# Ten elementwise instructions of the first stage move to GpSimd: four weight sums and six squares

## The chip, the cores and the metric

The kernel runs on one core of a Trainium2 chip. Such a core has five engines that work side by side, each through its own list of instructions in order: TensorE (PE, with its weight loads PEld), VectorE (DVE), ScalarE (ACT), GpSimd (POOL) and SyncE (SP), which here only issues transfers. They meet through semaphores. Operands lie in SBUF (on-chip memory, 128 partitions) or in PSUM, into which PE writes. The metric is the time of one execution on the device in microseconds (us).

## The reference

A decoder trunk of two layers on 512 tokens of width 1024, float32, each layer being `h += 0.5*FFN1(rms(h)); h += Mixer(rms(h)); h += 0.5*FFN2(rms(h))`, and a last normalisation. The first mixer is attention beside a convolution, the second a gated DeltaNet. The part that matters is the very first feed-forward network and its normalisation:

```
def rms_norm(x, g):
    y = xf * lax.rsqrt(jnp.mean(xf * xf, axis=-1, keepdims=True) + NORM_EPS)
    return (y * g).astype(x.dtype)

def swiglu_ffn(h, w_in, w_out):
    gate, up = jnp.split(h @ w_in, 2, axis=-1)
    return (jax.nn.silu(gate) * up) @ w_out
```

with `w_in` of 1024 x 5632 and `w_out` of 2816 x 1024.

## The kernel before

**Layout.** The input stands transposed, features on partitions: `h[d]`, d = 0..7, is a tile of 128 features x 512 tokens. The factor 1/rms of a token (`R`) is multiplied in after the first product, so the product with the weights can start before it is known; only the gain is multiplied in before.

**Split products.** PE multiplies in a faster format (fp32r), and to keep float32 accuracy each operand is split into a rounded part (hi, made by ACT) and a remainder (lo = value - hi, made by DVE). A product takes three matmuls: hi*hi, hi*lo, lo*hi (`mm3`, lines 144 to 146). Weights are split in `wsplit`: ACT makes `whi` (line 120), DVE `wlo` (line 121).

**Fewer products by sums.** A feed-forward network's first product is computed in seven block products where eight would be usual, from sums of blocks (Strassen-Winograd). The sums of x blocks are made in `Norm.sums`, the sums of weight blocks in `sums12` and `sums34`, once for each of the 22 iterations f of the loop over `block(f)`; those of f+1 while f is multiplied. For the first network the weights of f = 0 are fetched ahead, among the x tiles, into four tiles named `raw_pre`, and `sums12(0)` and `sums34(0)` run in the first stage. Each makes two 128x512 instructions, lines 399, 400 and 405, 406, on DVE. They form a chain: 405 needs 400, and 406 needs 399 and 405. ACT needs the result of 405 for its second `whi`, whose `wlo` follows on DVE.

**The first stage**, `Norm.start`, takes the x tiles in four pairs k (d = 2k even, 2k+1 odd):

- ACT multiplies in the gain (`gain`, line 249): `xe` from the even tile, `xo` from the odd one.
- DVE makes sums of 128x256 blocks (lines 256, 260, 262, 263).
- ACT rounds to `xh` (line 271; 128x512 for the even, 128x1280 for the odd tile), DVE subtracts to `xl` (line 276).
- ACT squares `h[d]` into a temporary tile (line 230): tag `a` with two buffers for even d, tag `sq` with one buffer for odd d. PE sums the square over its partitions (line 232, four matmuls of one column for each tile), for 1/rms.
- PE runs ten small matmuls (`warm`, line 209), for the first three pairs, whose result is not used.

Between the pairs `step(ahead)` runs pieces of the first network's generator: the `wsplit`s of f = 0, `sums12(0)` and `sums34(0)`. Then `block(0)` follows, in which `scale` turns the sums into 1/rms.

**What sets the order.** The lists of PE, ACT and DVE in the first stage and in the network's loop are ordered by the code (`manual_schedule`); POOL's and SP's, and all lists in the mixers, are ordered by a scheduler when the program is built. The tile pools add waits: a buffer is written again only when its readers are through. The buffers of `raw_pre` are taken next by the fetches for f = 1, and the pool of the x parts `xe` and `xo` gives its memory to the third weight tile of f = 1.

## Time and profile before

| | |
|---|---|
| median of 3 runs | 2079.42 us (2076.62 to 2080.59) |
| the profiled execution | 2078.23 us |
| its span, first to last instruction | 2076.5 us |
| mean granted TensorE clock | 0.979 |
| mean of a square, ACT line 230 (128x512), 8 of them in the first stage | 615 and 616 ns |
| mean of a weight sum, DVE lines 399, 400, 405, 406 (128x512) | 684 to 692 ns |
| mean of `xl` on DVE, 128x512 and 128x1280 | 686 and 1492 ns |
| mean of `xh` on ACT, 128x512 and 128x1280 | 626 and 1258 ns |
| DVE waits in the first 32.4 us | 3.1 us for `xh`, 2.6 us for the first `xe`, 1.8 us for `whi` |

A profile row of instructions in order of time reads: start, length (us), engine, line, operation, output<-inputs, shape, count, and in brackets the idle time of the engine ahead of it and what ended it. Instructions of one engine overlap a little, since the next begins while the last one drains; the distance from start to start tells what one costs in a row of them. A group's row has the busy time, then the mean in ns, then idle time and releasers. Buffer numbers are left out of names.

### The profile page before, as it was taken

To read this page: it belongs to the slowest core of one execution; us is meant where nothing else is said; L and a number is where in the kernel's file an instruction comes from. 1 tells how busy PE (TensorE), PEld (TensorE's weight loads), DVE (VectorE), ACT (ScalarE), POOL (GpSimd) and SP (SyncE) were. 2 spreads that over 40 slices of the span, in tenths; PEclk is the share of its full clock that TensorE was granted. 3 is DMA by queue.
4 is the path that set the end of the run, shared out by engine and by line. 5 is a ranking of instruction groups with operands and counts; after the bars stand their busy time and mean duration, and the time that the engine had idled before them with its cause. 6 is when DMAs were issued, how large, how long until landed. Compare 5 with 4: busy or idle time off the path is not lost.

```text
span 2076.5 us, 32975 instructions
## 1 busy us (share of the span) xinstructions
PE 2006.1 (97%) x12692; PEld 1774.8 (85%) x12692; DVE 1610.2 (78%) x2761; ACT 1114.4 (54%) x1985; POOL 134.0 (6%) x191
## 2 busy tenths in 40 slices
PE   7999999999999999999999999979989999999997
PEld 6999997786578999987999998767778888999986
DVE  7888879797568888889888888657685578888876
ACT  6444457546654444465444446686454754444455
POOL 0000000110000000000000000233312220000000
PEclk9999999999799999999999999989989999999998
DMA  4333332784043333322333332679634563333321
GB/s 138 111 103 106 103 101 93 178 193 93 21 107 115 108 104 102 97 87 83 113 105 102 102 102 83 180 220 233 140 117 122 122 142 107 103 105 108 98 86 46
DMA packets 108845, 237.70 MB, mean 114 GB/s; under 512 B 22160, under 2 KB 24976, under 8 KB 108688
## 3 DMA queue, kind: packets, MB, share of 16 engines
q1 hardware_dynamic: 90544, 193.06, 30.2%
q0 software_dynamic: 17616, 42.02, 10.8%
q8 instruction: 99, 1.62, 0.3%
q10 hardware_dynamic: 528, 0.52, 0.1%
q14 instruction: 58, 0.48, 0.1%
HBM read 224.55 MB, written 11.01 MB: 113 GB/s over the span
## 4 chain that ended last, share of the span: by engine, by line
PE 80%; DVE 10%; issue 5%; ACT 3%; DMA 2%; SPq 0%; POOL 0%; DVEq 0%; ACTq 0%; POOLq 0%
PE mm L145 12%; PE mm L146 12%; PE mm L144 12%; PE sc L145 7%; PE sc L144 7%; PE sc L146 7%; PE po L146 2%; PE po L145 2%; PE po L144 2%; PE tr L144 2%; PE tr L146 2%; PE tr L145 2%; DVE wlo L121 1%; DVE gl L433 1%; DVE sb L1227 1%
## 5 line engine op out<-in xcount | busy, mean ns | idle before, releaser
L121 DVE TENSOR_TENSOR wlo<-raw,whi 128x1024 fp32r<-128x1024 f32 (+1 forms) x400 | 473.7, 1202 | 158.4 <-ACT whi L120 154.3
L144 PE MATMUL mm<-xh,whi 128*128 128x256 f32 (+2 forms) x1800 | 559.2, 311 | 5.4 <-ACT b L469 3.0
L146 PE MATMUL mm<-xh,wlo 128*128 128x256 f32 (+2 forms) x1800 | 555.5, 309 | 3.3 <-DMA wlo<-in_wgdn 3.3
L145 PE MATMUL mm<-xl,whi 128*128 128x256 f32 (+2 forms) x1800 | 553.9, 308 | 0.8 <-DVE xl L276 0.8
L120 ACT ACTIVATE whi<-raw 128x1024 fp32r<-128x1024 f32 (+1 forms) x400 | 404.8, 1034 | 40.8 <-issue 14.4
L144 PEld LDWEIGHTS mm<-xh,whi 128*128 128x128 f32 (+1 forms) x1800 | 342.0, 190 | 38.4 <-ACT b L469 5.6
L145 PEld LDWEIGHTS mm<-xl,whi 128*128 128x128 f32 (+1 forms) x1800 | 341.7, 190 | 27.4 <-DVE xl L276 1.3
L146 PEld LDWEIGHTS mm<-xh,wlo 128*128 128x128 f32 (+1 forms) x1800 | 342.0, 190 | 20.4 <-DMA wlo<-in_wgdn 3.7
L144 PE MATMUL sc<-xh,whi 128*128 128x256 f32 x1056 | 299.4, 283 | 7.9 <-DVE b L505 7.9
L145 PE MATMUL sc<-xl,whi 128*128 128x256 f32 x1056 | 298.3, 283 | 0.0
L146 PE MATMUL sc<-xh,wlo 128*128 128x256 f32 x1056 | 298.2, 282 | 0.0
L144 PEld LDWEIGHTS sc<-xh,whi 128*128 128x128 f32 x1056 | 201.9, 191 | 9.6 <-DVE b L505 9.6
L433 DVE TENSOR_TENSOR gl<-g,gh 128x512 fp32r<-128x512 f32 (+1 forms) x286 | 179.2, 647 | 32.2 <-ACT gh L432 29.9
L432 ACT ACTIVATE gh<-g 128x512 fp32r<-128x512 f32 (+1 forms) x286 | 166.3, 592 | 67.1 <-PE mm L145 34.8
L146 PEld LDWEIGHTS sc<-xh,wlo 128*128 128x128 f32 x1056 | 202.0, 191 | 0.0
L145 PEld LDWEIGHTS sc<-xl,whi 128*128 128x128 f32 x1056 | 202.0, 191 | 0.0
L450 ACT ACTIVATE a<-a 128x512 f32<-128x512 f32 x88 | 55.6, 632 | 256.8 <-DVE a L449 256.8
L130 ACT ACTIVATE whi<-raw 128x512 fp32r<-128x512 f32 (+2 forms) x109 | 77.1, 735 | 97.1 <-PE mm L145 70.7
L486 ACT ACTIVATE b<-mm 128x256 f32<-128x256 f32 x88 | 33.8, 384 | 162.7 <-PE mm L146 162.7
L501 ACT ACTIVATE b<-mm 128x256 f32<-128x256 f32 x88 | 33.8, 385 | 136.9 <-PE mm L146 136.9
L145 PE MATMUL mm<-gl,whi 128*128 128x512 f32 (+1 forms) x220 | 82.8, 376 | 4.9 <-DVE gl L433 4.7
L826 DVE SCALAR_TENSOR_TENSOR cv<-pad,prm_t,cv 128x512 f32<-128x512 f32 x120 | 84.0, 755 | 0.8
(421 smaller groups left out, 3538.5 us busy)
## 6 DMA issues: line engine op xcount, KB each, us to landing
raw<-in_wf1i SPq DMA_DIRECT2D x82, 512.0 KB, 3.5
raw<-in_wf2i SPq DMA_DIRECT2D x82, 512.0 KB, 3.5
raw<-in_wgdn SPq DMA_DIRECT2D x32, 512.0 KB, 4.9
wlo<-in_wgdn POOLq DMA_DIRECT2D x64, 256.0 KB, 5.8
raw<-in_wf2i SPq DMA_DIRECT2D x56, 256.0 KB, 2.6
raw<-in_wf1i SPq DMA_DIRECT2D x52, 256.0 KB, 2.7
raw<-in_wf1b SPq DMA_DIRECT2D x20, 512.0 KB, 3.5
raw<-in_wf2b SPq DMA_DIRECT2D x20, 512.0 KB, 3.5
```

The lines of the kernel that those rows point to most:

```text
L120: A.activation(hi[:, s], src[:, s], AF.Copy)
L121: V.tensor_sub(lo[:, s], src[:, s], hi[:, s].bitcast(F32))
L130: A.activation(hi[:, s], raw[:, s], AF.Copy)
L144: PE.matmul(ps, whi, xhi, start=first, stop=False, skip_group_check=skip)
L145: PE.matmul(ps, whi, xlo, start=False, stop=False, skip_group_check=skip)
L146: PE.matmul(ps, wlo, xhi, start=False, stop=last, skip_group_check=skip)
L432: A.activation(hi, g[f][:, s], AF.Copy)
L433: V.tensor_sub(lo, g[f][:, s], hi.bitcast(F32))
L450: A.activation(cg[f], cg[f], AF.Silu)
L486: A.activation(b0[f][:, HT:], pb[f][:, :HT], AF.Copy)
L501: A.activation(b1[f][:, :HT], pb[f][:, :HT], AF.Copy)
L826: V.scalar_tensor_tensor(acc, x, w, acc, op0=ALU.mult, op1=ALU.add)
```

## The change

In the first network alone, the four weight sums of f = 0 are issued to POOL instead of DVE. In `Norm.start`, the squares of the first three pairs (d = 0 to 5) are made by a multiplication `h*h` on POOL instead of ACT's Square; those of the last pair stay on ACT.

```diff
@@ -227,7 +227,10 @@
                 for d in (e, o):
                     sq = tmp("sq" if d % 2 else "a", 1 + (d + 1) % 2)
-                    A.activation(sq, h[d], AF.Square)
+                    if k < 3:
+                        G.tensor_mul(sq, h[d], h[d])
+                    else:
+                        A.activation(sq, h[d], AF.Square)
                     for c in range(NT):
                         PE.matmul(self.st[:, c * NK + d:c * NK + d + 1], sq[:, c * P:(c + 1) * P], o1,
                                   start=True, stop=True)
@@ -396,14 +399,16 @@
             def sums12(f):
                 if f < NF:
                     x, y, z, w = wa[f]
-                    V.tensor_sub(z[:, q2], x[:, q2], y[:, q1])
-                    V.tensor_add(y[:, q1], y[:, q1], w[:, q1])
+                    eng = V if f or not xn.first else G
+                    eng.tensor_sub(z[:, q2], x[:, q2], y[:, q1])
+                    eng.tensor_add(y[:, q1], y[:, q1], w[:, q1])
 
             def sums34(f):
                 if f < NF:
                     x, y, z, w = wa[f]
-                    V.tensor_sub(y[:, q2], y[:, q1], x[:, q2])
-                    V.tensor_sub(w[:, q2], z[:, q1], y[:, q2])
+                    eng = V if f or not xn.first else G
+                    eng.tensor_sub(y[:, q2], y[:, q1], x[:, q2])
+                    eng.tensor_sub(w[:, q2], z[:, q1], y[:, q2])
```

POOL's list after the first memset, with the change (the squares are line 231, the sums lines 403, 404, 410, 411; `a_129` and `sq_135` are the squares of the first pair, `a_165` and `sq_171` of the second, `a_207` and `sq_213` of the third):

```order
L231 ISA
L231 TENSOR_TENSOR a_129<-h_71 128x512
L231 TENSOR_TENSOR sq_135<-h_73 128x512
L231 TENSOR_TENSOR a_165<-h_77 128x512
L231 TENSOR_TENSOR sq_171<-h_79 128x512
L403 TENSOR_TENSOR raw_pre_91<-raw_pre_75,raw_pre_81 128x512
L231 TENSOR_TENSOR a_207<-h_83 128x512
L404 TENSOR_TENSOR raw_pre_81<-raw_pre_81,raw_pre_85 128x512
L410 TENSOR_TENSOR raw_pre_81<-raw_pre_81,raw_pre_75 128x512
L411 TENSOR_TENSOR raw_pre_85<-raw_pre_91,raw_pre_81 128x512
L231 TENSOR_TENSOR sq_213<-h_87 128x512
```

Before, the next instruction of POOL after that memset was a transfer of the second stage. The row ISA stood ahead of POOL's first multiplication in the DeltaNet stage, and is there no longer.

PE's list in the first stage, before (line 232: sums over a square; 209: the warming matmuls; `mm_275` with `whi_187` is the first weight product, one triple for each pair of x tiles):

```order
L209 MATMUL po_108<-xh_110 128x512 x10
L144 MATMUL mm_275<-xh_110,whi_187 128x256
L145 MATMUL mm_275<-xl_111,whi_187 128x256
L146 MATMUL mm_275<-xh_110,wlo_188 128x256
L144 MATMUL mm_275<-xh_121,whi_187 128x256
L145 MATMUL mm_275<-xl_122,whi_187 128x256
L146 MATMUL mm_275<-xh_121,wlo_188 128x256
L144 MATMUL mm_275<-xh_157,whi_187 128x256
L145 MATMUL mm_275<-xl_158,whi_187 128x256
L146 MATMUL mm_275<-xh_157,wlo_188 128x256
L232 MATMUL tr_107<-cst,a_207 128x1 x4
L232 MATMUL tr_107<-cst,sq_213 128x1 x4
```

And at the same place now:

```order
L209 MATMUL po_108<-xh_110 128x512 x10
L235 MATMUL tr_107<-cst,a_207 128x1 x4
L235 MATMUL tr_107<-cst,sq_213 128x1 x4
L209 MATMUL po_108<-xh_110 128x512 x10
L144 MATMUL mm_275<-xh_110,whi_187 128x256
L145 MATMUL mm_275<-xl_111,whi_187 128x256
L146 MATMUL mm_275<-xh_110,wlo_188 128x256
```

The first nine weight matmuls now stand behind the sums over the third pair's squares, and behind the last ten warming matmuls; the triple of the fourth pair (`xh_199`) follows them in both.

In the DeltaNet stage, the scheduler's order moved too. PE's list at the third pair's inverse, before (`tr_15718`, `tr_15732`, `tr_15738` and the 64x64 rows are steps of the inverse; `mm_16350` and `mm_16388` are projections for gates, 24 matmuls each):

```order
L1278 MATMUL tr_15718<-Vb_15702,s_15704 128x128 x4
L1278 MATMUL tr_15725<-Vb_15708,s_15710 128x128 x4
L146 MATMUL mm_16350<-xh_13393,wlo_16354 128x512
L144 MATMUL mm_16350<-xh_13539,whi_16353 128x512
L145 MATMUL mm_16350<-xl_13540,whi_16353 128x512
L146 MATMUL mm_16350<-xh_13539,wlo_16354 128x512
L1284 MATMUL tr_15732<-s_15723,s_15714 128x128 x4
L144 MATMUL mm_16350<-xh_13561,whi_16353 128x512
L145 MATMUL mm_16350<-xl_13562,whi_16353 128x512
L146 MATMUL mm_16350<-xh_13561,wlo_16354 128x512
L144 MATMUL mm_16388<-xh_13072,whi_16391 128x512
L1284 MATMUL tr_15738<-s_15730,s_15716 128x128 x4
```

And now:

```order
L146 MATMUL mm_16388<-xh_13539,wlo_16392 128x512
L1283 MATMUL tr_15718<-Vb_15702,s_15704 128x128 x4
L1283 MATMUL tr_15725<-Vb_15708,s_15710 128x128 x4
L144 MATMUL mm_16388<-xh_13561,whi_16391 128x512
L145 MATMUL mm_16388<-xl_13562,whi_16391 128x512
L146 MATMUL mm_16388<-xh_13561,wlo_16392 128x512
L1289 MATMUL tr_15732<-s_15723,s_15714 128x128 x4
L1289 MATMUL tr_15738<-s_15730,s_15716 128x128 x4
```

All of `mm_16350` and 21 of the 24 matmuls of `mm_16388` now stand ahead of the inverse. Before, 23 of `mm_16388` were spread over the inverse and the scan behind `tr_15738`. In the same stage DVE's 31 substitution steps for the second half of the heads (lines 1227 and 1228, multiplication and reduction) began among the steps of the second pair's inverse; now the first of them stands behind that pair's square root.

## The prediction

> **What bounds the kernel now.** I read the page's top rows first, then windows over the stage that the change touches, then the chain of waits up to 45 us, then VectorE (DVE) instruction by instruction.

> ```profile
> span 2076.5 us, 32975 instructions
> ...
> PE 2006.1 (97%) x12692; PEld 1774.8 (85%) x12692; DVE 1610.2 (78%) x2761; ACT 1114.4 (54%) x1985; POOL 134.0 (6%) x191
> ```

> TensorE (PE) is busy 97% of the span, and nothing that the change does alters its work. So the change is worth what it does to the moment from which PE runs without a break. GpSimd (POOL) has 134 us of work in the whole kernel.

> ```profile
> 5.90:32.40 26.50, 21.48 (x127) 19.59 (x128) 21.10 (x33) 19.42 (x28) 0.00 (x0) 1.00 0.38 128
> ...
> 27.50:57.00 29.50, 27.03 (x211) 25.22 (x209) 23.71 (x43) 16.66 (x25) 0.00 (x0) 1.00 0.43 138
> ```

> In these windows the columns after the length are PE, weight loads, DVE, ACT, POOL. From 27.5 us on PE is busy 27.0 of 29.5 us. Ahead of it stands the first stage, where DVE works 21.1 of 26.5 us and POOL nothing.

> ```profile
> 28.95 1.44 DVE xl L276
> 30.41 4.99 DMA raw<-in_wf1i
> 35.49 0.70 DVE raw L400
> ```

> The chain runs through the last xl (the remainder of the x tiles): its end frees the memory into which the next weights are fetched, 4.99 us later DVE adds them, and PE waits behind that. A shift of this xl shifts everything after it. Now DVE itself:

> ```profile
> 5.91 0.43 DVE L256 TENSOR_TENSOR xe<-xe 128x256 f32<-128x256 f32 x1 [2.59 <-ACT xe L249]
> ...
> 9.75 1.49 DVE L276 TENSOR_TENSOR xl<-xo,xh 128x1280 fp32r<-128x1280 f32 x1 [1.51 <-ACT xh L271]
> 11.16 0.42 DVE L256 TENSOR_TENSOR xe<-xe 128x256 f32<-128x256 f32 x1
> 11.68 0.43 DVE L260 TENSOR_TENSOR xo<-xo,xe 128x256 f32<-128x256 f32 x1
> 12.02 0.42 DVE L262 TENSOR_TENSOR xo<-xo,xe 128x256 f32<-128x256 f32 x1
> 12.36 0.42 DVE L263 TENSOR_TENSOR xo<-xo 128x256 f32<-128x256 f32 x1
> 12.69 0.69 DVE L276 TENSOR_TENSOR xl<-xe,xh 128x512 fp32r<-128x512 f32 x1
> 14.17 1.49 DVE L276 TENSOR_TENSOR xl<-xo,xh 128x1280 fp32r<-128x1280 f32 x1 [0.79 <-ACT xh L271]
> 16.35 0.69 DVE L121 TENSOR_TENSOR wlo<-raw_pre,whi 128x512 fp32r<-128x512 f32 x1 [0.68 <-ACT whi L120]
> 16.96 0.68 DVE L399 TENSOR_TENSOR raw_pre<-raw_pre,raw_pre 128x512 f32<-128x512 f32 x1
> 17.68 0.69 DVE L400 TENSOR_TENSOR raw_pre<-raw_pre,raw_pre 128x512 f32<-128x512 f32 x1
> 18.29 0.42 DVE L256 TENSOR_TENSOR xe<-xe 128x256 f32<-128x256 f32 x1
> ...
> 22.65 0.69 DVE L405 TENSOR_TENSOR raw_pre<-raw_pre,raw_pre 128x512 f32<-128x512 f32 x1
> 23.37 0.69 DVE L406 TENSOR_TENSOR raw_pre<-raw_pre,raw_pre 128x512 f32<-128x512 f32 x1
> 24.46 1.22 DVE L121 TENSOR_TENSOR wlo<-raw_pre,whi 128x1024 fp32r<-128x1024 f32 x1 [0.40 <-ACT whi L120]
> ...
> 27.07 0.69 DVE L276 TENSOR_TENSOR xl<-xe,xh 128x512 fp32r<-128x512 f32 x1
> ...
> 28.89 1.49 DVE L276 TENSOR_TENSOR xl<-xo,xh 128x1280 fp32r<-128x1280 f32 x1
> ```

> The six rows from 11.16 on are one group (a pair of x tiles); there are four. Start to start, a 128x256 instruction takes 0.34, the 128x512 xl 0.60, the 128x1280 xl 1.41 us (9.75 to 11.16). All of them read two operands from SBUF.

> **What goes.** On DVE, L399 and L400 go: 16.96 to 18.29 is 1.33 us. L405 and L406 go, and with them the wait for the ACT instruction behind them: 22.65 to 24.46 is 1.81 us. ACT loses six squares, so it has whi ready earlier, and the pause ahead of 16.35 goes too (the group ends at 14.17 + 1.41 = 15.58): 0.77 us. Together 3.91 us, all on the chain. That is the whole gain, if the ten new POOL instructions disturb nobody.

> **What comes, and what it does to DVE.** POOL gets ten 128x512 instructions, in the order shown above: four squares, one sum, a square, three sums, the last square. The nearest rows are those of the later stage, by shape, and one meeting of the two engines:

> ```profile
> L1249 POOL TENSOR_TENSOR qe<-qe,qT 128x512 f32<-128x512 f32 x8 | 11.3, 1407 | 2.8 <-ACT qT L1092 2.8
> L1271 POOL TENSOR_TENSOR s<-s,gcst 128x512 f32<-128x512 f32 x8 | 10.3, 1283 | 49.0 <-PE tr L1100 23.5 <-DMA s<-Ld 14.3 <-PE sc L1317 6.8
> ```

> ```profile
> 1438.60 0.17 DVE L1227 TENSOR_TENSOR sb<-sb,lb 128x18 f32<-128x18 f32 x1
> ...
> 1439.28 1.21 DVE L1227 TENSOR_TENSOR sb<-sb,lb 128x21 f32<-128x21 f32 x1
> ```

> ```profile
> 1439.10 1.34 POOL L1249 TENSOR_TENSOR qe<-qe,qT 128x512 f32<-128x512 f32 x1
> ```

> A DVE instruction with two SBUF operands takes 0.17 us alone, and 1.21 us when it is issued 0.18 us into a POOL multiplication. It ends at 1440.49, that is, it began about 0.12 us before POOL's recorded end (1440.44). So the two do not run side by side: DVE waits for the POOL instruction. I count a hold of 1.28 - 0.13 = 1.15 us for each of the ten. In the first stage every DVE instruction is of this kind, so the two engines take turns:

> - The first square starts when the first x tile has landed, as ACT's first instruction does:

> ```profile
> 5.15 0.72 ACT L249 ACTIVATE xe<-h,prm_t 128x512 f32<-128x512 f32 x1 [2.91 <-DMA h<-in_x]
> ```

> - That is 5.15, so DVE's first instruction starts at 5.15 + 1.15 = 6.3, not 5.91.
> - Squares two and three fall between the four short DVE instructions. The fourth square writes the buffer of the second, and waits for PE's sums over it:

> ```profile
> 10.90 1.87 PE L232 MATMUL tr<-cst,a 128*128 128x1 f32 x8 [10.90 <-ACT a L230]
> ...
> 12.63 1.84 PE L232 MATMUL tr<-cst,sq 128*128 128x1 f32 x8
> ```

> - Two such sums take 12.63 + 1.84 - 10.90 = 3.6 us. After the first square at 6.5 they end near 10.1. The even xl ends there too, at 10.5; the fourth square then holds the pair of engines to 11.65, and the big xl runs 11.65 to 13.05 instead of 9.75 to 11.16: DVE is 1.9 us late.
> - In the second group six DVE instructions (4 x 0.34 + 0.60 + 1.41 = 3.4 us) alternate with the six POOL instructions that are left (6 x 1.15 = 6.9 us). 13.05 + 10.3 = 23.3 instead of 15.58: **7.7 us late**. ACT's xh, for which DVE now waits 0.79 us, are made in POOL's turns.
> - From there POOL is silent, and DVE gets the 3.91 us back. The last xl ends 7.7 - 3.9 = **3.8 us late**, at 34.2 instead of 30.4.

> Bounds: 3.9 us gained if squares did not hold DVE. On the other side each hand-over could cost 0.1 to 0.2 us more than the bare durations (1.34 and the mean of 1.41 above 1.28): 5.8 us lost. I take 3.8, the value by the rows that show the hold. ACT's lost squares (0.5 us each) count for nothing more, since ACT then waits for DVE. The load for the next iteration that waits for L405 is released earlier; that for y follows wlo, later by the same 3.8, and is needed after the 4.99 us transfer.

> **An instruction of POOL that moves.** Ahead of the first POOL multiplication the order has an extra instruction (ISA); it stood in the later stage.

> ```profile
> 1425.95 0.12 POOL L1082 MEMSET pad<- 128x3 f32 x1
> 1426.58 1.26 POOL L1249 TENSOR_TENSOR qe<-qe,qT 128x512 f32<-128x512 f32 x1 [0.51 <-ACT qT L1092]
> ```

> There it fits into 0.51 us in which POOL waited for ACT anyway. At the start it stands before the first x lands at 5.15, so I count nothing for it. [...]

> **PE in the first stage.** PE's order now has the sums over the sixth tile's square, and ten warming matmuls, ahead of the first weight matmuls. By the turns above that square ends near 21.9.

> ```profile
> 25.12 2.56 PE L209 MATMUL po<-xh 128*128 128x512 f32 x10
> ```

> Sums (0.9), these ten (2.56) and nine weight matmuls (27.03 / 211 = 0.13 each) end near 26.4. The next needs the fourth even xl: 27.07 + 0.69 + 3.8 = 31.6. That is no loss of itself, but a pause of some 5 us, where before there was none. What PE does after a pause:

> ```profile
> 1530.17 0.39 PE L1331 MATMUL po<-vn,at 128*128 128x128 f32 x2
> ...
> 1534.29 0.79 PE L1331 MATMUL po<-vn,at 128*128 128x128 f32 x2 [3.28 <-DVE vn L1330]
> ...
> 1540.51 0.38 PE L1331 MATMUL po<-vn,at 128*128 128x128 f32 x2
> ```

> After 3.28 us idle the same matmul takes 0.79 instead of 0.39, and 0.38 again at 1540.5: some 6 us at half speed, 3 us lost. Here 0 to 2.4 us, since 0.65 of it falls into a wait that PE has anyway:

> ```profile
> 38.63 0.39 PE L144 MATMUL sc<-xh,whi 128*128 128x256 f32 x1 [0.65 <-DVE b L505]
> ```

> The pause of 3.28 us came after a stretch with gaps, this one comes after dense matmuls. I take the middle, **1.1 us**. [...]

> **Order changes in the DeltaNet stage.** There the scheduler decides, and the order moved. Some 20 matmuls of a gate projection, which filled pauses of the third pair's inverse and scan, now stand ahead of them.

> ```profile
> 1610.00:1620.00 10.00, 10.00 (x46) 8.04 (x45) 4.21 (x10) 7.81 (x19) 3.59 (x5) 1.00 0.66 160
> ```

> At 10 / 46 = 0.22 us, 20 fillers are 4.4 us: the most that is lost if the pauses stay empty. Against this, DVE's substitution steps now begin behind the second pair's inverse, so that the 3.28 us wait for vn above shrinks, by 3.3 at best. I take **+0.7 us**.

> **Sum.** 3.8 + 1.1 + 0.7 = 5.6 us slower. Against the profiled execution (2078.23 us, of which 2076.5 are span) that is 2083.8. The runs shown have a median of 2079.42 (2076.62 to 2080.59), so the profiled one lies inside them, 1.2 below; from the median the sum gives 2085.0. I say **2084**.

> **Rivals.**
> [...]
> - *POOL loses the turns*: back-to-back DVE instructions keep POOL out, and it only works in DVE's pauses. The last square then ends near 29, and PE's chain (0.9 + 2.56 + 1.2 us) near 33.7, some 2 later than in the forecast: 2086. Or hand-overs cost 0.2 each, with the same time.
> - *It cancels*: fewer of the ten meet DVE, since part of them falls into ACT's waits, and half of the 7.7 is lost: within 1 us of no change, 2079.

> **How the numbers follow.** Forecast 0.60 (+2.5 to +9 around 5.6), no hold 0.13, POOL loses the turns 0.15, it cancels 0.12. A measurement here tells about 0.2%, 4.2 us, from no change. Slower by more: 0.42 of the forecast and 0.13 of the lost turns, 0.55. Faster by more: half of the no-hold case and a little for the later order, 0.09. The rest, 0.36, within. The range from 2075.5 to 2089 takes in both ends of each bound but the worst sums.

> **What would show it.** In the profile after: DVE's first xe instruction near 6.3, and 128x256 rows of 0.8 to 1.5 us among the first twelve; the second 128x1280 xl ending near 23 (before 15.7), the fourth near 34; after 23 us no long DVE rows. PE's warming matmuls end near 25, with a pause up to 31. If those DVE rows stay at 0.42 with POOL busy beside them, the hold is wrong, and the kernel is faster. If the first stage is as forecast and the time is not, the order in the DeltaNet stage (1480 to 1610 us) is what I mis-sized.

## The result and the profile after

| | before | after |
|---|---|---|
| median, 4 executions each | 2080.01 us (2076.62 to 2081.58) | 2090.66 us (2089.76 to 2094.72) |
| the profiled execution | 2078.23 us | 2091.35 us |
| its span | 2076.5 us | 2089.5 us |

The change made the kernel slower: ratio **1.0056, interval 1.0040 to 1.0072**. A repeat on another chip (10 executions) gave a median of 2091.12 and a ratio of 1.0039 (1.0023 to 1.0054). The direction was as predicted, the size lies outside the predicted range (2075.5 to 2089.0).

The three later sessions ran before 77 times: mean 2081.9, from 2074.2 to 2088.8, standard deviation 3.4. All 14 executions of after have a mean of 2090.2. So the change costs **8.4 +- 1.6 us**, and the execution of before against which the sum was made, 2078.23, lay 3.6 below that mean. Differences of means below are taken with the 95% error of the executions' scatter.

First the page of after, its head:

```profile
span 2089.5 us, 32982 instructions
...
PE 2012.6 (96%) x12692; PEld 1781.8 (85%) x12692; DVE 1617.6 (77%) x2757; ACT 1111.1 (53%) x1979; POOL 147.6 (7%) x201
```

PE has the same 12692 instructions, and 6.5 us more of busy time: of the 13.0 us of span one half is idle time, the other matmuls that took longer. Then the windows over the first stage (after the length: PE, weight loads, DVE, ACT, POOL, then the granted clock):

```profile
5.64:32.39 26.75, 23.55 (x105) 20.70 (x105) 24.81 (x27) 15.69 (x22) 12.97 (x10) 0.85 0.34 111
27.50:57.00 29.50, 26.40 (x174) 25.24 (x172) 22.17 (x43) 16.04 (x23) 0.00 (x0) 0.83 0.37 117
```

The granted clock was 1.00 in both windows before; now it is 0.85 and 0.83. These means need care: the trace records the clock stretch by stretch, the first record starts at 17.74 us in before and at 13.88 in after, and what lies ahead of it counts as 1.00. The matmuls there run at half speed in both (the first ten warming matmuls take 4.11 us in before and 4.61 in after, the second ten 2.52 and 2.56). So the two profiles differ in clock from some 14 us on: before stays at full speed from 17.74, after falls to half speed at 20.71 and again at 30.95. DVE is busy for longer, 24.8 us with 27 instructions against 21.1 with 33. DVE in order of time shows why:

```profile
5.64 0.55 DVE L259 TENSOR_TENSOR xe<-xe 128x256 f32<-128x256 f32 x1 [2.38 <-ACT xe L252]
6.30 1.07 DVE L263 TENSOR_TENSOR xo<-xo,xe 128x256 f32<-128x256 f32 x1
...
7.63 1.26 DVE L266 TENSOR_TENSOR xo<-xo 128x256 f32<-128x256 f32 x1
...
14.59 1.48 DVE L265 TENSOR_TENSOR xo<-xo,xe 128x256 f32<-128x256 f32 x1
15.99 1.51 DVE L266 TENSOR_TENSOR xo<-xo 128x256 f32<-128x256 f32 x1
17.43 1.77 DVE L279 TENSOR_TENSOR xl<-xe,xh 128x512 fp32r<-128x512 f32 x1
19.12 2.32 DVE L279 TENSOR_TENSOR xl<-xo,xh 128x1280 fp32r<-128x1280 f32 x1
...
22.76 0.42 DVE L265 TENSOR_TENSOR xo<-xo,xe 128x256 f32<-128x256 f32 x1
...
30.90 1.49 DVE L279 TENSOR_TENSOR xl<-xo,xh 128x1280 fp32r<-128x1280 f32 x1
```

And POOL beside it:

```profile
9.67 1.04 POOL L231 TENSOR_TENSOR sq<-h 128x512 f32<-128x512 f32 x1 [1.07 <-PE tr L235]
10.67 2.53 POOL L403 TENSOR_TENSOR raw_pre<-raw_pre,raw_pre 128x512 f32<-128x512 f32 x1
...
15.87 1.35 POOL L410 TENSOR_TENSOR raw_pre<-raw_pre,raw_pre 128x512 f32<-128x512 f32 x1
17.30 1.35 POOL L411 TENSOR_TENSOR raw_pre<-raw_pre,raw_pre 128x512 f32<-128x512 f32 x1
18.61 1.49 POOL L231 TENSOR_TENSOR sq<-h 128x512 f32<-128x512 f32 x1
```

While POOL works, a 128x256 instruction of DVE that meets one of POOL's takes 1.1 to 1.5 us (the first of all 0.55), and 0.42 once POOL is silent. From 15.87 on the starts alternate strictly: POOL 15.87, DVE 15.99, POOL 17.30, DVE 17.43, POOL 18.61, DVE 19.12. POOL is stretched too: the sum at 10.67 lies beside two long DVE instructions (1.78 us from 10.28, 1.50 from 11.98) and takes 2.53 us. The second big `xl` ends at 21.44, 5.8 us later than before; the last one at 32.39, 2.0 later than the 30.38 of before. PE:

```profile
20.15 1.38 PE L235 MATMUL tr<-cst,sq 128*128 128x1 f32 x8 [1.26 <-POOL sq L231]
21.39 4.61 PE L209 MATMUL po<-xh 128*128 128x512 f32 x10
...
28.81 0.38 PE L144 MATMUL mm<-xh,whi 128*128 128x256 f32 x1 [0.99 <-ACT xh L274]
29.82 0.39 PE L145 MATMUL mm<-xl,whi 128*128 128x256 f32 x1 [0.63 <-DVE xl L279]
...
31.24 0.41 PE L146 MATMUL sc<-xh,wlo 128*128 128x256 f32 x1
...
41.59 0.28 PE L146 MATMUL mm<-xh,wlo 128*128 128x256 f32 x1
```

The third ten warming matmuls take 4.61 us, where the same ten took 2.56 before, and from 31.0 to 41.0 us a weight matmul stands with 0.41 instead of 0.28: half speed. The pauses here are short: 1.26 us for POOL's last square, then 0.99 and 0.63 us. The slow warming matmuls fill most of the pause that the prediction expected.

The rest of the time comes later. One and the same DVE instruction at the end of the second stage (start, length), before and after:

```profile
384.09 0.43 DVE L799 CAST qa<-qa 128x512 f32<-128x512 int32 x1 [1.86 <-DMA qa<-in_pos]
```

```profile
389.55 0.43 DVE L804 CAST qa<-qa 128x512 f32<-128x512 int32 x1 [1.87 <-DMA qa<-in_pos]
```

That is +5.5. Another one stands ahead of the DeltaNet heads, and a third behind their scan; before:

```profile
1343.93 0.18 DVE L1138 SCALAR_TENSOR_TENSOR g<-p__2319_13667,ea 128x32 f32<-128x32 f32 x1
...
1638.96 0.35 DVE L1314 SCALAR_TENSOR_TENSOR r__2992_16734<-sc,ksc,vb 128x128 f32<-128x128 f32 x1
```

and after:

```profile
1348.66 0.18 DVE L1143 SCALAR_TENSOR_TENSOR g<-p__2319_13667,ea 128x32 f32<-128x32 f32 x1
...
1651.89 0.35 DVE L1319 SCALAR_TENSOR_TENSOR r__2992_16734<-sc,ksc,vb 128x128 f32<-128x128 f32 x1
```

+4.7 and +12.9: between `g` and `r`, the stretch in which nothing of the code was edited takes 8.2 us more, and 13.0 is the whole. The 90 us that end 2 us before `r` hold the third and fourth pair of heads (length, PE busy, clock), before and after:

```profile
1546.96:1636.96 90.00, 89.96 (x521) 0.96 0.60 141
```

```profile
1559.89:1649.89 90.00, 87.35 (x506) 0.96 0.59 138
```

Before, PE never waited there; now it does for 2.7 us. PE's waits between 1390 and 1640 us, by what ended them (us in total, times, longest), before:

```profile
PE po L1331 <- DVE vn L1330: 3.3, 1, 3.3
...
PE tr L1284 <- DVE s L1280: 2.7, 4, 0.8
...
PE tr L1100 <- issue: 0.6, 1, 0.6
```

and after:

```profile
PE tr L1105 <- DVE s L1258: 3.7, 1, 3.7
PE tr L1289 <- DVE s L1285: 3.5, 5, 0.8
PE po L1336 <- DVE vn L1335: 2.9, 1, 2.9
...
PE tr L1105 <- issue: 1.9, 4, 0.9
```

The wait for `vn`, which was to shrink by up to 3.3 us, shrank by 0.33 (3.28 to 2.95 at the instruction). Among the rows left out, the wait for a `wlo` from memory shrank too (3.3 to 2.3); the other large ones grew.

### The profile page after: what moved, and what is told of

The parts are those of the page before. It is cut to its first block, busy times and chain, and to the rows that moved or that the text cites. A ratio compares the mean times of both kernels' runs of the same rounds, so it can differ in the third digit from the quotient of the medians.

```text
span 2089.5 us, 32982 instructions
## 1 busy us (share of the span) xinstructions
PE 2012.6 (96%) x12692; PEld 1781.8 (85%) x12692; DVE 1617.6 (77%) x2757; ACT 1111.1 (53%) x1979; POOL 147.6 (7%) x201
## 4 chain that ended last, share of the span: by engine, by line
PE 79%; DVE 9%; issue 5%; ACT 3%; DMA 3%; SPq 0%; POOL 0%; DVEq 0%; ACTq 0%; POOLq 0%
PE mm L145 12%; PE mm L144 12%; PE mm L146 12%; PE sc L145 7%; PE sc L144 7%; PE sc L146 7%; PE po L146 2%; PE po L145 2%; PE po L144 2%; PE tr L144 2%; PE tr L146 2%; PE tr L145 2%; DVE wlo L121 1%; DVE gl L438 1%; PE tr L1105 1%
## 5 line engine op out<-in xcount | busy, mean ns | idle before, releaser
L121 DVE TENSOR_TENSOR wlo<-raw,whi 128x1024 fp32r<-128x1024 f32 (+1 forms) x400 | 473.6, 1202 | 158.7 <-ACT whi L120 154.5
L144 PE MATMUL mm<-xh,whi 128*128 128x256 f32 (+2 forms) x1800 | 560.4, 311 | 6.3 <-ACT b L474 3.0
L120 ACT ACTIVATE whi<-raw 128x1024 fp32r<-128x1024 f32 (+1 forms) x400 | 404.6, 1033 | 41.4 <-issue 14.4
L144 PEld LDWEIGHTS mm<-xh,whi 128*128 128x128 f32 (+1 forms) x1800 | 343.3, 191 | 39.7 <-ACT b L474 5.5
L144 PE MATMUL sc<-xh,whi 128*128 128x256 f32 x1056 | 299.7, 284 | 8.4 <-DVE b L510 8.4
L144 PEld LDWEIGHTS sc<-xh,whi 128*128 128x128 f32 x1056 | 202.2, 191 | 9.9 <-DVE b L510 9.9
```

Source lines behind the costliest of these rows:

```text
L120: A.activation(hi[:, s], src[:, s], AF.Copy)
L121: V.tensor_sub(lo[:, s], src[:, s], hi[:, s].bitcast(F32))
L144: PE.matmul(ps, whi, xhi, start=first, stop=False, skip_group_check=skip)
```

## The experiments

Three questions were open: whether the hold of DVE is the loss; why the first stage shows +5.5 with the last `xl` only 2.0 late; and whether the DeltaNet stage's 8.2 us belong to the change or to chance. In the program order of all these kernels but the last the DeltaNet stage takes one of two forms. The ISA row of the change is the load of POOL's instruction library; in the lists of these kernels it stands ahead of POOL's first multiplication or addition. Where it stands in the DeltaNet stage the lists are those of before, and where it stands in the first stage those of after, whichever part of the change put it there. This is the **later order** below.

**Load early.** The only edit to before, ahead of the first stage:

```diff
+    from concourse import library_config
+    G.load_library(library_config.standard)
```

> The kernel before with one thing added: POOL's library load (the ISA instruction) is asked for at the start, as the change does without saying so; nothing else is new, sums and squares stay where they were. The scheduler then gives the DeltaNet stage instruction for instruction the order it has after the change. Theory A (order): of the 13.0 us between the two profiled spans 5.5 stand in the first 50 us and the rest, 7.5, comes from this order alone; so the first stage stays as before and the time is 7.5 us above before, by +6 to +9 us, about 2087.5, and all of it between 1425 and 1610 us. Theory B (lateness): the DeltaNet stage loses because the work arrives 5.5 us later there, or because POOL is busy early on; then this run is within 1.5 us of before. Theory C (my prediction's size): +0.7 us.

Measured: ratio 1.0025 (1.0008 to 1.0041), a mean of +5.2 us over its session's before (12 executions). The first stage is undisturbed (its last `xl` ends at 29.59 in the profile), and the same 90 us as above, ending 2 us ahead of `r`, read:

```profile
1550.29:1640.29 90.00, 87.85 (x496) 0.92 0.58 135
```

So PE's waits in the later order are not a matter of chance. A repeat on another chip:

> The kernel before with the library load alone asked for at the start, a second time, since its twelve times fell into two heaps (2077.5 to 2083.6 and 2089.5 to 2093.7) that a single profile cannot tell apart. Theory 'order': mean again 4 to 6 us above that of before, with the pauses at the third pair and the wait for s in the profile. Rival 'the heaps were a draw': within 2 us of before.

Measured: ratio 1.0035 (1.0018 to 1.0052), +6.9 us. Both together: **+6.0 +- 2.2 us** for 24 executions, without an edit to a single arithmetic instruction. The executions of the first session fall into two heaps, 2077.5 to 2083.6 (six) and 2089.5 to 2093.7 (six).

A second profile of the kernel before:

> The kernel before itself, for a second profile of it. The one that my prediction started from took 2078.23 us and had 30.7 us of half speed in the DeltaNet stage; three kernels with the same order there had 47.8. Theory 'the profile of before was a lucky one': this one shows 40 us or more of half speed there and a DeltaNet stage 4 to 9 us longer. Rival: 27 to 34 us of half speed and the stage within 2 us of the first profile.

Measured: 2084.18 us, with the last `xl` ending at 30.52. Yet the DVE and ACT instructions between 100 and 300 us start 3.1 us later (median) than in the first profile. This goes with the moment at which PE first gets its full clock: by the clock records from 17.7 us on in the first profile and only from 26.8 on in the second, where the second ten warming matmuls are still at half speed (2.52 us in the first profile):

```profile
22.18 4.61 PE L209 MATMUL po<-xh 128*128 128x512 f32 x10
```

The two profiles with the load early, whose first stage is that of before, go the same way: full clock from 18.0 us on and starts 1.0 us earlier, full clock from 27.8 on and starts 3.7 us later. So the first profile was a lucky one; a shift of 3 to 4 us in the first stage is within what one kernel does by itself.

The verdict on the order rests on one measure taken in all the profiles with one of the two orders: the length from `g` to `r` as quoted above, and PE's idle time in it (the length less PE's busy time in that window). The kernels that are not told yet follow below:

| profile | order | g to r, us | PE idle in it | PE idle in the last 90 |
|---|---|---|---|---|
| before | earlier | 295.0 | 20.6 | 0.0 |
| before again | earlier | 296.7 | 18.7 | 0.0 |
| no sums | earlier | 303.0 | 19.5 | 0.0 |
| no sums, warmed | earlier | 303.2 | 22.6 | 0.0 |
| copies | earlier | 303.8 | 21.2 | 0.0 |
| load early | later | 301.7 | 26.2 | 2.2 |
| load early again | later | 305.9 | 24.7 | 2.4 |
| sums only | later | 302.5 | 28.0 | 2.2 |
| squares only | later | 304.8 | 23.4 | 2.7 |
| squares again | later | 308.2 | 26.1 | 2.4 |
| after | later | 303.2 | 26.3 | 2.7 |
| after again | later | 301.5 | 24.7 | 2.6 |
| filled | later | 303.7 | 24.2 | 2.7 |

Idle time separates the two orders without exception: means of 20.5 and 25.4, **4.9 us more**. The lengths scatter by 9 us within one order, since between 1420 and 1640 us the matmuls that show half speed sum to 31 us in the first profile of before and 37 to 48 in the others of the earlier order. A length less its idle time and half of that half-speed time lies between 257 and 261 us in all thirteen. So the idle time is the order's, and the scatter of the lengths is largely the clock's.

**One part of the change alone.** The sums on POOL, the squares left on ACT:

```diff
+                    eng = V if f or not xn.first else G
+                    eng.tensor_sub(z[:, q2], x[:, q2], y[:, q1])
...
```

> Only the four sums go to POOL, the six squares stay on ACT. Theory A: the order of the DeltaNet stage is that of after (+7.5 us). In the first stage DVE saves the 3.1 us of the four sums and pays four holds of 0.6 to 1.15 us: -0.7 to +1.5 us there, PE without the long half-speed stretch; in all +7 to +9 us. Rival (the sums are what costs, the squares cost nothing): +11 to +13 us, as after.

Measured: ratio 1.0030 (1.0017 to 1.0044), +6.6 us: no more than the load alone gives. Its last `xl` ends at 32.28. And the squares on POOL, the sums left on DVE:

```diff
+                    if k < 3:
+                        G.tensor_mul(sq, h[d], h[d])
+                    else:
+                        A.activation(sq, h[d], AF.Square)
```

> Only the six squares go to POOL, the four sums stay on DVE. Theory A: the order of the DeltaNet stage is that of after (+7.5 us). In the first stage six POOL instructions hold DVE; after lost 5.8 us on DVE by the end of its second group with ten of them, 0.58 each, so six cost 3.5 less the 0.8 us of ACT's wait: the last xl ends 2 to 3.5 us later than before, and with some half-speed PE behind it the first 50 us lose 2 to 5 us. In all +9.5 to +12.5 us. Rival: the squares read one tile twice and hold nobody; then DVE's first group runs as before (first big xl at 9.75 us) and the first stage gains 0.8.

> The six squares alone on POOL, a second time, since four times (2092.5 to 2106.1) are few. By addition of the parts (order +5, first stage +3.6 as with the copies, the hold of a multiplication on top 0 to 2) it should lie 8 to 11 us above before, about 2091. Rival: squares without the sums are worse than both together, +14 us or more, through a first stage in which PE's pause is longer.

Measured: 1.0096 (1.0070 to 1.0122) with 4 executions, and 1.0048 (1.0031 to 1.0064) with 9 on another chip, +10.4 us. Both together lie 6.9 +- 3.3 above the load alone, after itself 2.4 +- 2.4 above it. So of the two parts, taken singly, the squares are the one that costs beyond the order; why they cost more alone than together with the sums, with the last `xl` at 31.9 in both profiles, these runs don't tell.

**What the removal is worth.** The four sums of the first iteration left out, in before; the load and the order stay where they were:

```diff
+            if d > 1:
+                nc.gpsimd.memset(raw[:, T:], 0.0)
...
+                    if f or not xn.first:
+                        V.tensor_sub(z[:, q2], x[:, q2], y[:, q1])
...
```

> The four weight sums of iteration 0 are left out altogether (the blocks they would fill are set to zero by POOL before the first x tile lands); squares as before, and the order of the DeltaNet stage as before. This is the most that taking the sums from DVE could ever bring. Theory (DVE's chain bounds the first stage): the last xl ends 3.1 us earlier (1.33 + 1.81) and the time falls by 2.5 to 3.1 us, to about 2077. Rival (PE, with its warming matmuls and the first weights, bounds it): 0 to -1 us.

The memsets fill what the sums would have written; POOL is through with them at 2.2 us, before the first x lands. Measured: ratio 1.0009 (0.9994 to 1.0024). **Nothing is gained.** PE in the first stage, then DVE:

```profile
15.18 4.61 PE L211 MATMUL po<-xh 128*128 128x512 f32 x10
22.86 4.61 PE L211 MATMUL po<-xh 128*128 128x512 f32 x10
```

```profile
24.70 1.23 DVE L123 TENSOR_TENSOR wlo<-raw_pre,whi 128x1024 fp32r<-128x1024 f32 x1 [2.46 <-ACT whi L122]
...
29.14 1.49 DVE L278 TENSOR_TENSOR xl<-xo,xh 128x1280 fp32r<-128x1280 f32 x1
```

Both groups of warming matmuls ran at half speed (4.61 for 4.11 and 2.52 in the first profile of before), the square's buffer came free later, ACT's square and `whi` with it, and DVE waited 2.46 us: the last `xl` ends at 30.63, where it ended before. The missing sums need not be the cause of the slow matmuls: the second profile of before has the same two groups at 4.61, with the full clock from 26.8 us on (here 27.5) and its last `xl` ending at 30.52. To take the slow matmuls away, the same with six warming matmuls more, right behind the first `xh`:

```diff
+                warm(6 if k == 0 else 0)
```

> As the run without the four sums (they are left out, and the blocks that they would fill are zero), and PE begins warming 3 to 4 us earlier, with six more warming matmuls as soon as the first xh is there. That run had gained nothing: ACT waited for PE, which ran its warming at half speed until 27.3 us (18.2 in before). Theory 'PE's clock, not DVE, is the next bound of the first stage': with PE at full speed by 16 us the saving of the sums appears, 2 to 3 us off before. Rival 'the sums are hidden anyway': again within 1 us of before.

Measured: the last `xl` ends at 28.34, 2.0 us earlier than in before, and the ratio is 1.0003 (0.9989 to 1.0017). The full clock comes at 18.9 us here, nearly as early as in the first profile of before, and DVE's and ACT's instructions between 100 and 300 us start 0.6 us earlier than there. So of 2.0 us on the last `xl` 0.6 arrive in the profile, and nothing that can be measured in the times; whatever bounds the kernel there next, it isn't this `xl`.

**One operand instead of two.** Before with copies on POOL in place of the six squares, which leaves the squares out and keeps the earlier order:

```diff
+                        G.tensor_copy(sq, h[d])
```

> The six squares are replaced by six plain copies on POOL (one SBUF operand each; the squares of the first six x tiles are left out), the sums stay on DVE. A copy asks for no library, so the DeltaNet stage keeps the order of before. Theory 'every POOL instruction that reads SBUF holds DVE': DVE's first two groups show rows of 0.8 to 1.5 us beside the copies, the first stage loses 2 to 5 us as the run with squares alone did (4.9), and the time is +2 to +5 us. Rival 'only POOL instructions with two operands hold': DVE rows stay at 0.42 us, the first stage gains up to 0.8 us, the time is -0.8 to 0.

Measured: ratio 1.0019 (1.0003 to 1.0034), +3.9 +- 2.4 us against the 77 executions. POOL and DVE meet here as well, POOL first, then DVE:

```profile
5.92 0.61 POOL L231 COPY sq<-h 128x512 f32<-128x512 f32 x1
7.27 0.88 POOL L231 COPY a<-h 128x512 f32<-128x512 f32 x1 [0.74 <-DMA h<-in_x]
```

```profile
6.03 0.79 DVE L259 TENSOR_TENSOR xe<-xe 128x256 f32<-128x256 f32 x1 [2.69 <-ACT xe L252]
...
7.60 0.83 DVE L266 TENSOR_TENSOR xo<-xo 128x256 f32<-128x256 f32 x1
```

A copy holds DVE too, for a shorter time than a multiplication does: these 128x256 instructions take 0.79 to 0.83 us, those of after 1.07 to 1.51. DVE recovers (last `xl` 30.74, +0.4), and still the kernel is slower. What differs in the first stage is PE's pause and the clock behind it:

```profile
27.16 0.39 PE L144 MATMUL mm<-xh,whi 128*128 128x256 f32 x1 [3.89 <-ACT xh L274]
28.17 0.58 PE L145 MATMUL mm<-xl,whi 128*128 128x256 f32 x1 [0.62 <-DVE xl L279]
28.55 0.41 PE L146 MATMUL mm<-xh,wlo 128*128 128x256 f32 x1
```

By the clock records PE goes to half speed at 27.6 us, shortly after it resumes, for 10.2 us. That this is the price of the copies is not shown: the instructions between 100 and 300 us start 3.9 us later than in the first profile of before, but those of before itself and of the load early reached 3.1 and 3.7.

**After again, and its pause filled.**

> The changed kernel itself once more, for a second profile and a dozen times beside those of the others. The profiles so far show that the DeltaNet stage's own time moves by some 8 us from one execution to the next with the share of it that PE spends at half speed (30.7 us of half speed in the profile of before, 47.8 in the run without sums, which has the same instruction order there). Theory A: the change costs about 5 us by the DeltaNet stage's order (the run with the library load alone: +4.3) and 5 to 6 us in the first stage, +10 us in the median, with a spread of 10 us between executions. Rival: the 10.65 us were a draw of four executions, and a dozen give +5, the order alone.

Measured: ratio 1.0039 (1.0023 to 1.0054), as told above. In this profile the third ten warming matmuls kept full speed, so the pause has its full length, and 3.4 us at half speed follow:

```profile
21.28 2.54 PE L209 MATMUL po<-xh 128*128 128x512 f32 x10
29.03 0.38 PE L144 MATMUL mm<-xh,whi 128*128 128x256 f32 x1 [4.14 <-ACT xh L274]
```

Filling it with warming matmuls (six between the third pair's sums, sixteen behind):

```diff
+                    warm(16)
                     step(ahead)
...
+                    if d == 5:
+                        warm(6)
```

> The changed kernel with more warming matmuls where PE paused in it: six between the two sums of the third pair (it waited 1.26 us for the last square there) and sixteen more ahead of the first weight matmuls (then 0.99 and 0.63 us for the fourth pair). Nothing else. Theory 'the pauses cost the clock': the third warming group runs at 0.21 us a matmul instead of 0.42, the stretch of half-speed matmuls from 31.0 to 41.1 us goes, and of the 5.5 us that the first 50 us lost 2.0 stay (DVE's lateness): about 3.5 us faster than after. Rival 'the clock falls for another reason, or DVE's lateness alone sets the end': no gain, or a loss of up to 3 us by the added matmuls.

Measured: the pause falls to 0.52 us and the warming matmuls from the second ten on run at full speed, and the ratio is 1.0045 (1.0028 to 1.0061): no faster than after. So filling the pause wins nothing back; 3.4 us at half speed follow in this profile too, from 34.5 us on.

**The moved gate put back.** After, with the second gate projection of the third pair held behind the inverse's second product, near where it stood before:

```diff
+                    if hd == 5:
+                        with tc.issue_after(zi[p].ins):
+                            gate(hd)
```

> The changed kernel with one part of the DeltaNet order put back: the 24 matmuls of the second gate projection of the third pair are queued behind the inverse's second product again, as before the change, where they fill PE's pauses. Theory 'the empty pauses': the waits of 0.78, 0.3, 0.6, 0.25, 0.16 and 0.2 us at the third pair (2.3 to 2.6 us in every profile with the new order, none with the old) go, and with them the one or two stretches of 3.4 us at half speed around 1600 to 1635 us: 2.5 to 5 us faster than the changed kernel's 2089.7 (mean of ten), about 2086. Rival 'the early part of that stage (the wait of 1.3 to 3.7 us for s, 1445 to 1456 us) carries the loss': the time stays within 1 us.

Measured: ratio 1.0068 (1.0045 to 1.0090), 5.6 +- 3.6 us slower than the 14 executions of after. The pauses in the scan are filled, and others open ahead of them, on PE:

```profile
1576.52 1.13 PE L1283 MATMUL tr<-Vb,s 128*128 128x128 f32 x8 [2.71 <-DMA Vb<-Vd]
...
1580.45 2.08 PE L1289 MATMUL tr<-s,s 128*128 128x128 f32 x8 [0.79 <-DVE s L1285]
```

In after, where the gate stands ahead, PE's waits for `Vb` sum to 1.5 us; here they sum to 4.5, the longest 2.71, and PE then works at half speed (2.08 for 1.13 us). As a repair the edit failed. It shows that this stage's order alone, with the load and the first stage as in after, moves the time by 5.6 +- 3.6 us.

No version was found that beats before.

## Why the prediction was half right

The forecast was 5.6 us slower: 3.8 from DVE, 1.1 from PE, 0.7 from the order, on a base of 2078.23. Measured against the 77 executions it is 8.4. The sum came as near as that by luck: its first stage is 2.8 us too large and its order 5.3 too small. Point by point:

- **DVE's hold (3.8).** The mechanism is right: first rows of 1.07 to 1.5 us, strict turns, 0.42 when POOL is silent. The size was too large: DVE was 0.8 us late at the end of the first group instead of 1.9, and 5.8 at the end of the second instead of 7.7. The first instruction (0.55 us) was hardly held, and some of POOL's work fell into DVE's waits for `xh`. After that DVE won back 3.8 of the forecast 3.9, so the last `xl` came 2.0 late, not 3.8.
- **What goes (3.91).** It came back on DVE's chain, but it was counted as time. Of the 3.91 the sums make 3.1, and without them the kernel is not faster (0.9994 to 1.0024), nor with the last `xl` 2.0 us earlier. The step "a shift of this xl shifts everything after it" holds at most for delays.
- **PE's pause (1.1).** Seen in after again: 4.14 us where 5 were foretold, and 3.4 us at half speed behind it. Against the first profile of before its price would be 0.8 us (after again: first stage +2.8 less the 2.0 of `xl`) to 3.5 (after: 5.5 less 2.0), but that profile had the early full clock. For the first stage as a whole, four profiles with the first stage of before stand at 0, +3.1, -1.0 and +3.7 against the first profile (before, before again, load early, again), mean +1.5, and four with that of after at +5.5, +2.8, +3.5 and +2.5 (after, again, filled, gate back), mean +3.6. That is a net **2.1 +- 2.6 us**, against 4.9 in the forecast, and no more than the 2.0 by which the `xl` is late: a price of the pause by itself is not shown.
- **The order in the DeltaNet stage (0.7): the step that failed.** I wrote "4.4 us: the most that is lost if the pauses stay empty", and against this a wait for `vn` that "shrinks, by 3.3 at best", and took +0.7. Measured with the load moved and this order alone: **+6.0 +- 2.2**. The pauses did stay empty (2.2 to 2.7 us in eight of eight profiles of the later order, 0.0 in five of five of the earlier one), inside my bound. The `vn` wait shrank by 0.33, so hardly anything stood against them. And PE idles some 2.5 us more elsewhere in that stretch, in after among `s` and `issue` waits (3.7 and 1.9 us for 0.5 and 0.6) that I had not counted at all. Why `vn` gained so little: SP's list now has three fetches of weights, and not two, right ahead of the transfers for the substitution, `lb` among them. First those fetches, before and after, then the issues of `lb` from the view of that tile, before and after:

```profile
1456.20 7.00 SPq L112 DMA_DIRECT2D raw<-in_wgdn  x2
```

```profile
1464.75 13.30 SPq L112 DMA_DIRECT2D raw<-in_wgdn  x3
```

```profile
L1222 SPq DMA_DIRECT2D lb<-Ld x8: 326/492/811, 1469.7 to 1493.7; - x8
```

```profile
L1227 SPq DMA_DIRECT2D lb<-Ld x8: 393/484/1621, 1484.7 to 1503.5; - x8
```

The `lb` issues begin 15.0 us later, where `g` is 4.7 later. The prediction took up PE's and DVE's lists and not SP's. That the third fetch is the cause was read from the order and these rows; it was not tried by itself.

- **The moved ISA row (nothing).** As an instruction it costs nothing that the profiles show: with it alone at the start the last `xl` ends at 29.59 us, not later than the 30.38 of before, and in after the first square started at 4.87, when its x tile had landed. But its place is what decides the order, and I treated the two as separate entries.
- **The base.** 2078.23 lies 3.6 below the mean of 77 executions.

In retrospect 2081.9 + 6.0 + 2.1 = 2090.0, and the mean measured is 2090.2. The terms come from separate runs, each with an error of 2 us or more, so the close fit is partly luck.

Of the other cases that were given a chance, *no hold* fell with DVE's first rows (1.07 us at 6.30, where such a row takes 0.42 once POOL is silent). *POOL loses the turns* fell too: the last square ended at 20.1, not near 29. *It cancels* had a true core, fewer meetings than I counted, and lost by the order.

**What stays open.** The early load and the later order always came together here, so a cost of the load's place by itself, in some way that the profile doesn't show, is not excluded; the table's idle time speaks for the order, and accounts for 4.9 of 6.0 us. How an execution comes by its share of half speed in the DeltaNet stage, and with it the two heaps of times, is not settled. Nor is what makes the copies slower, or what bounds the first stage once its last `xl` is earlier.

## What to carry to other kernels

Before moving work to an idle engine, measure whether its instructions hold up those of the busy one: here ten POOL instructions and DVE's held each other up in turns (1.07 to 1.51 us for 0.42 on DVE, 2.53 for 1.28 on POOL), and work taken off DVE brought nothing that could be measured, since DVE's end was not what the time hung on (a last `xl` 2.0 us earlier, ratio 1.0003). Where a scheduler orders part of the program, read its new lists for every engine and transfer queue, far from the edit too; one moved setup instruction changed the order of a stage 1400 us later, and the kernels with that alone lose 6.0 of the 8.4 us. And take a base from many executions: one profiled execution was 3.6 us off the mean, nearly half of the effect.
